# Narrow expert's tiles first in the experts' pool, and the first gate input split inside the GLU

## The chip, the cores and the metric

The kernel runs on one core of a Trainium2 chip. The metric is the device time of one execution in microseconds (us). The engines are TensorE (PE, with its weight loads PEld), VectorE (DVE), ScalarE (ACT), GpSimd (POOL) and SyncE (SP). Here SP and POOL start the DMA transfers, each in its own queue; the gathers by an index table are started by POOL.

## The reference

One layer of a decoder trunk, 2048 tokens of width 1024, float32:

```
h   = RMSNorm(x)
[u | q | k | v] = h @ W_in
yA  = S5 state-space model on u, GELU, then y * sigmoid(y @ w_glu + b_glu)
yB  = causal sliding-window attention (128) on q, k, v, 8 heads, sinks, relative bias
g   = sigmoid(h @ W_gate + b)
x  += (gA * (yA @ W_A) + gB * (yB @ W_B)) @ W_out
x  += HierMoE(RMSNorm(x))       32 experts of width 512, two per token
x  += (p @ W_ple) * sigmoid(RMSNorm(x) @ W_pg + b)
out = RMSNorm(x)
```

An attention step computes s = 0.125 * scores + bias, m = max(max(s), sink), exp(s - m) with its sum, and divides by the sum plus exp(sink - m).

## The kernel before

Every matrix product is made of three matmuls (lines 73 to 75): each float32 operand is split into a rounded high half (a cast on ACT) and a low half (a subtraction on DVE), and the products high x high, low x high and high x low are added up in PSUM. So every matrix that comes from memory costs a load, an ACT cast and a DVE subtraction before PE can use it.

The stages follow each other in program order, each overlapping the next at its edges: the u projection (to 122 us), q, k and v with pieces of the S5 model (to 343), the GLU (to 397), the gates' branch A (426 to 775), branch B (to 1048), the output projection (to 1257), the routing tables with the last pieces of the p projection (to 1300), the experts (1323 to 2084), and the last residual with its norm (to 2308).

- **Order.** A tile framework fixes each engine's instruction order when the program is built. Instructions of one engine, and the DMA starts of one queue, run in that order.
- **Memory.** Tiles live in pools; pools stack up from the left and from the right end of SBUF. A pool that is opened where another was closed takes its place, and a tile waits only for the work on those earlier tiles whose bytes it takes. Inside a pool the tiles lie in the order in which they are first asked for. The same tag with `bufs=n` rotates over n places.
- **u projection** (`u_mm`). Per block of 256 tokens, `scale` makes the row norms `rp` by a matmul (L459), copies them from PSUM to `rb` (ACT, L460, 8 of them), stores `rb`, and the eviction multiplies the block's products by `rb` into `ut` (DVE, L465). The q, k, v units are told to stay behind `self.scaled`, the last scaling instructions. The x halves for the next block are `xh` (ACT, L417) and `xl` (DVE, L418).
- **GLU and attention** (`phase_mix`). `weave` runs a generator of main steps and, after each, a fraction of steps of a second generator. The GLU has 16 steps (4 column blocks c, 4 output blocks m); its result goes into `ys` (L613), which is stored by 8 transfers after the last step (L619: one by SP, seven by POOL). The attention has 32 steps, 16 pairs of 128-token blocks and 2 key heads; 0.4 of a step runs per GLU step, 1.2 per step of branch A. In an attention step DVE takes the max of the scores (L820), ACT the exponentials with their sums (L829), DVE the reciprocal (L831), and POOL multiplies (L832). m, es and dn are tiles of 4 numbers per partition with two places each.
- **Gates, branch A** (`gates(c2, 0, 1)`). 32 steps: 2 halves of the columns, 8 token blocks e, 2 column groups. A step takes 48 matmuls `gz` (h times the gate weights gA) and 24 matmuls `gb` (y times bA), then tanh into `th` (ACT), the product into `mo` (DVE), and a store. For the first block both `gz` products come ahead of the `gb` products. The h halves come from `load_halves` (two loads, two casts, two subtractions per block; tiles `gh0000`, `gh0001` for the first block, whose raw loads go into a raw pool apart), the y halves `gy` from the stored `ys`. The first block's halves are asked for after the GLU's pools are closed. The gates' pools pB and pBh are opened on the left side where the GLU's lay; pB's first tiles, `bgate` among them, lie on `ys`.
- **Experts** (`moe`). 16 pairs of a wide expert (more than 128 token rows) and a narrow one. `moe_in` gathers the rows of one expert from memory into `xg` (L1356, tile names `xgs...`), PE transposes them (L1366, `txs`), ACT and DVE split them into `xw` (wide) or xh and xl (narrow). The gather's row numbers come from `row_index` (L1344 to L1348). After the first fetch all engines branch on a count (`overflow`, L1550). The experts' pool pM begins at byte 149,344 of a partition, worked out from the tile sizes; its tiles lie in the order of first use: `xw` (14,336 bytes), `xg` (2 of 4,096), then the rest. The three `po` tiles of the p projection before it, which are stored by `pp_d<-po` (L1070), were at 162,656 to 174,944.
- **Tail.** The pool of the last stage begins at the same byte 149,344; its first tile is `gtail` (8,192 bytes).

Of the kernel before, what the change touches and what calls it, by code (L numbers as in the profile page):

```python
# [11 lines left out]
F32 = mybir.dt.float32  # L12
F32R = mybir.dt.float32r
# [15 lines left out]
RM = 224  # L29
# [19 lines left out]
class Kern:  # L49
# [10 lines left out]
    @staticmethod  # L60
    def weave(main, fill, rate):

        due = 0.0
        for _ in main:
            due += rate
            while due >= 1.0:
                due -= 1.0
                if next(fill, "end") == "end":
                    due = -1e9
# [278 lines left out]
    def phase_mix(self):  # L348
        with ExitStack() as cA:
            att = self.attention(cA)  # L350
            with ExitStack() as c2:
                self.weave(self.glu(c2), att, 0.4)
            self.hlB = self.weight_pools()
            with ExitStack() as c2:
                self.weave(self.gates(c2, 0, 1), att, 1.2)
            for _ in att:
                pass
        with ExitStack() as c2:
            for _ in self.gates(c2, 1, 2):
                pass  # L360
# [75 lines left out]
    def u_mm(self, e, hk, ss, p1, p2, ps, wu, ut):  # L436
# [16 lines left out]
        def scale():  # L453
# [6 lines left out]
            self.scaled = dv.ins, nc.scalar.copy(rb, rp).ins  # L460
# [125 lines left out]
    def glu(self, ctx):  # L586
# [12 lines left out]
        for c in range(4):  # L599
# [7 lines left out]
            for m in range(4):  # L607
                z = ps.tile([128, 512], F32, tag="z", name=f"z{c}{m}")
                for k in range(4):
# [5 lines left out]
                                       in1=yk[:, m].rearrange("p (i n) -> p i n", i=4), op0=ALU.add, op1=ALU.mult)  # L615
                yield
# [101 lines left out]
    def attention(self, ctx):  # L718
# [80 lines left out]
        for e in range(8):  # L799
            (kh, kl), qs, vs, kn = nxt  # L800
            for w in range(2):
# [4 lines left out]
                for kv in range(2):  # L806
# [12 lines left out]
                    m = p.tile([128, 4], F32, tag="m", name=f"m{e}{w}{kv}")  # L819
# [4 lines left out]
                    es = p.tile([128, 4], F32, tag="es", name=f"es{e}{w}{kv}")  # L824
                    V.tensor_tensor(out=es, in0=sk, in1=m, op=ALU.add)
                    A.activation(es, es, AF.Exp)
                    dn = p.tile([128, 4], F32, tag="dn", name=f"dn{e}{w}{kv}")
# [15 lines left out]
    def gates(self, ctx, br, nb):  # L843
# [3 lines left out]
        hl = self.hlB  # L847
# [5 lines left out]
        ph = self.pool(ctx, "pBh", 1, side=side)  # L853
        ps = self.pool(ctx, "psB", nb, space=PSUM, side=side)
        bg = p.tile([128, 16], F32, name="bgate", bufs=1)
        nc.sync.dma_start(bg, I["b_gate"])
# [11 lines left out]
        if br == 0:  # L868

            pad = ph.tile([128, 4, 256], F32R, tag="hh", name="hpad", bufs=3)  # L870
            nc.gpsimd.memset(pad[0:1, 0, 0:1].bitcast(F32), 0.0)
        ahead = None if br else halves(0, 0, 0)
        wt = self.wB if br else weights(0)
        for h in range(2):
            for e in range(8):
# [3 lines left out]
                yh, yl = self.load_half(p if br else ph, ysrc, "y", f"gy{br}{h}{e}", nb, 2 if br else 0)  # L879
# [613 lines left out]
    def moe(self):  # L1493
        nc = self.nc
        self.yb_d = self.scratch("yb_d", [2 * T + 1, 1024])
        order = []
# [279 lines left out]
```

## Time and profile before

| | us |
|---|---|
| median of 3 runs | 2310.47 |
| lowest, highest | 2309.33, 2317.18 |
| the profiled execution | 2310.56 |
| its span | 2308.8 |
| PE busy in it | 2215.5 |
| DVE busy | 1659.7 |
| ACT busy | 1209.8 |
| POOL busy | 364.7 |
| mean granted clock of PE | 0.981 |

The span is the time from the first to the last recorded instruction; the execution's own time is 1.8 us longer. "Granted clock" is the share of TensorE's full speed that it was given. Idle time of an engine is put down to its releaser, the work whose end let it go on.

### The profile page before, as it was taken

To read this page: it belongs to the slowest core of one execution; us is meant where nothing else is said; L and a number is where in the kernel's file an instruction comes from. 1 tells how busy PE (TensorE), PEld (TensorE's weight loads), DVE (VectorE), ACT (ScalarE), POOL (GpSimd) and SP (SyncE) were. 2 spreads that over 40 slices of the span, in tenths; PEclk is the share of its full clock that TensorE was granted. 3 is DMA by queue.
4 is the path that set the end of the run, shared out by engine and by line. 5 is a ranking of instruction groups with operands and counts; after the bars stand their busy time and mean duration, and the time that the engine had idled before them with its cause. 6 is when DMAs were issued, how large, how long until landed. Compare 5 with 4: busy or idle time off the path is not lost. (4 is left out here: it accounts for less than half of the span.)

```text
span 2308.8 us, 38073 instructions
## 1 busy us (share of the span) xinstructions
PE 2215.5 (96%) x14524; PEld 1997.4 (87%) x14524; DVE 1659.7 (72%) x2915; ACT 1209.8 (52%) x2019; POOL 364.7 (16%) x282
## 2 busy tenths in 40 slices
PE   8889999899999999999999599999999999999997
PEld 8789997799999999998887488888898888887875
DVE  7878647888886434435666577787778888887997
ACT  6433335576665323322223466666667767764443
POOL 0043201221210000000001111122122211210212
PEclk9899999899999999999999799999999999999998
DMA  8485453644436456545553688889888998886562
GB/s 308 135 279 180 152 155 107 232 142 143 138 115 210 152 165 199 195 132 173 169 158 124 242 300 294 295 315 340 326 308 323 342 332 312 329 323 233 199 211 92
DMA packets 135321, 512.51 MB, mean 222 GB/s; under 512 B 16416, under 2 KB 34768, under 8 KB 107744
## 3 DMA queue, kind: packets, MB, share of 16 engines
q1 hardware_dynamic: 112544, 429.56, 54.6%
q0 software_dynamic: 22448, 80.23, 9.2%
q8 instruction: 115, 1.88, 0.3%
q14 instruction: 70, 0.57, 0.1%
q10 hardware_dynamic: 144, 0.26, 0.0%
HBM read 405.51 MB, written 101.20 MB: 219 GB/s over the span
## 5 line engine op out<-in xcount | busy, mean ns | idle before, releaser
L1481 DVE TENSOR_TENSOR e_l<-e_r,e_h 128x2048 fp32r<-128x2048 f32 x192 | 438.1, 2289 | 142.7 <-ACT e_h L1480 139.6
L1480 ACT CAST e_h<-e_r 128x2048 fp32r<-128x2048 f32 x192 | 366.5, 1910 | 140.5 <-PE ws L1405 39.9
L1405 PE MATMUL ws<-xw,e_h 128*128 128x320 f32 (+2 forms) x1024 | 290.5, 359 | 3.6 <-PEq L1550 3.6
L1406 PE MATMUL ws<-xw,e_l 128*128 128x160 f32 (+2 forms) x1024 | 251.8, 248 | 0.0
L1405 PEld LDWEIGHTS ws<-xw,e_h 128*128 128x128 f32 x1024 | 192.2, 189 | 7.6 <-issue 3.9
L1406 PEld LDWEIGHTS ws<-xw,e_l 128*128 128x128 f32 x1024 | 195.9, 192 | 0.0
L1356 POOL DMA_INDIRECT xgs<-h_d,rt x48 | 78.6, 1638 | 420.6 <-PE txs L1366 385.1
L1456 POOL DMA_INDIRECT yb_d<-yos,rt x48 | 79.9, 1664 | 214.3 <-DVE yos L1452 135.2
L832 POOL TENSOR_TENSOR s<-s,dn 128x1024 f32<-128x1024 f32 (+1 forms) x32 | 64.4, 2013 | 276.0 <-DVE dn L831 149.5
L75 PE MATMUL pz<-pg_h,pl 128*128 128x512 f32 (+1 forms) x264 | 103.1, 391 | 3.0 <-DVE pl L1611 3.0
L73 PE MATMUL gus<-e_h,xhs 128*128 128x512 f32 x256 | 102.9, 402 | 0.0
L75 PE MATMUL gus<-e_h,xls 128*128 128x512 f32 x256 | 102.7, 401 | 0.0
L73 PE MATMUL pz<-pg_h,ph 128*128 128x512 f32 (+1 forms) x264 | 101.6, 385 | 1.0 <-ACT ph L1610 1.0
L74 PE MATMUL gus<-e_l,xhs 128*128 128x512 f32 x256 | 101.6, 397 | 0.0
L74 PE MATMUL pz<-pg_l,ph 128*128 128x512 f32 (+1 forms) x264 | 101.3, 384 | 0.0
L73 PE MATMUL u<-xh,u_h 128*128 128x256 f32 x256 | 72.8, 291 | 18.5 <-DVE ut L465 9.8
L829 ACT ACTIVATE s<-s,m 128x256 f32<-128x256 f32 (+1 forms) x128 | 62.7, 492 | 36.5 <-DVE m L823 34.4
L74 PE MATMUL u<-xl,u_h 128*128 128x256 f32 x256 | 73.6, 291 | 0.0
L75 PE MATMUL u<-xh,u_l 128*128 128x256 f32 x256 | 72.8, 287 | 0.0
L1366 PE MATMUL txs<-ident,xgs 128*128 128x128 f32 (+3 forms) x384 | 48.8, 264 | 23.4 <-DMA xgs<-h_d,rt 22.8
L916 ACT ACTIVATE gt<-gz,bgate 128x256 f32<-128x256 f32 x128 | 53.4, 469 | 29.5 <-PE gz L75 26.2
L1366 PEld LDWEIGHTS txs<-ident,xgs 128*128 128x128 f32 (+3 forms) x384 | 40.8, 143 | 31.0 <-issue 27.3
(1489 smaller groups left out, 7366.5 us busy)
## 6 DMA issues: line engine op xcount, KB each, us to landing
e_r<-in_We SPq DMA_DIRECT2D x192, 1024.0 KB, 5.8
m_d<-mo SPq DMA_DIRECT2D x64, 256.0 KB, 3.7
yg<-yb_d SPq DMA_DIRECT2D x15, 1024.0 KB, 7.3
xt<-in_xT SPq DMA_DIRECT2D x16, 512.0 KB, 8.5
sq<-in_x SPq DMA_DIRECT2D x16, 512.0 KB, 5.4
m<-m_d SPq DMA_DIRECT2D x16, 512.0 KB, 5.0
xr<-in_x SPq DMA_DIRECT2D x16, 512.0 KB, 4.4
x_d<-xr POOLq DMA_DIRECT2D x16, 512.0 KB, 3.1
```

What stands on the lines that cost most here:

```text
L73: mm(out, ah, bh, start=start, stop=False)
L74: mm(out, ah, bl, start=False, stop=False)
L75: return mm(out, al, bh, start=False, stop=stop)
L829: A.activation(s[:, i], s[:, i], AF.Exp, bias=m[:, i:i + 1], accum_out=dn[:, i:i + 1])
L832: nc.gpsimd.tensor_tensor(out=s, in0=s, in1=dn.unsqueeze(2).to_broadcast([128, 4, n]), op=ALU.mult)
L1356: nc.gpsimd.indirect_dma_start(out=xg[0:rows], out_offset=None, in_=self.h2_d[:], in_offset=bass.IndirectOffsetOnAxis(ap=idx[0:rows], axis=0))
L1366: nc.tensor.transpose(tp[:, k], xg[0:rows, kk * 128:kk * 128 + 128], self.ident[0:rows, 0:rows])
L1405: mm(acc[b].rearrange("p (a n) -> p a n", a=2), wh[:, c:c + 128], xk, start=s, stop=False)
L1406: mm(acc[b][:, 0:n], wl[:, c:c + 128], xk[:, 0], start=False, stop=e)
L1456: nc.gpsimd.indirect_dma_start(out=self.yb_d[:], out_offset=bass.IndirectOffsetOnAxis(ap=d[0:rows], axis=0), in_=yo[0:rows], in_offset=None)
L1480: nc.scalar.copy(hi, raw)
L1481: nc.vector.tensor_tensor(out=lo, in0=raw, in1=hi, op=ALU.subtract)
```

## The change

Five edits:

1. In `u_mm.scale` the copy of `rp` to `rb` moves from ACT to DVE.
2. `weave` takes a set of steps: the attention now gets 0.5 step after each of the first 10 GLU steps and none in the last six (5 steps instead of 6 in all), and 1.2 steps after each step of branch A from the third on.
3. At GLU step 11, (c, m) = (2, 2), a pool `pAh` for h halves is opened on the right side, beside the attention's pool, and the first block's loads, casts and subtractions are issued there. Branch A uses that pool for all its h halves. The y halves move into pB, whose first tiles are now bgate, th, mo, half and a pad of 2,016 bytes, so that these lie on `ys` and the y halves begin where `ys` ends. The tile `hpad` and its memset are gone.
4. m, es and dn of an attention step become three parts of one tile `med` with one place (`bufs=1`).
5. `moe` asks first for the narrow expert's tiles (xh, xl, act, ah, al, aw: 29,696 bytes), so that `xw` and `xg` lie that much further on. Worked out from the sizes, they are then at 179,040 to 201,568, where the tables of the routing were.

```diff
--- before.py
+++ after.py
@@ -58,10 +58,12 @@
         return ctx.enter_context(self.tc.tile_pool(**kw))
 
     @staticmethod
-    def weave(main, fill, rate):
+    def weave(main, fill, rate, steps=range(1 << 20)):
 
         due = 0.0
-        for _ in main:
+        for n, _ in enumerate(main):
+            if n not in steps:
+                continue
             due += rate
             while due >= 1.0:
                 due -= 1.0
@@ -348,11 +350,13 @@
     def phase_mix(self):
         with ExitStack() as cA:
             att = self.attention(cA)
+            cB = ExitStack()
             with ExitStack() as c2:
-                self.weave(self.glu(c2), att, 0.4)
+                self.weave(self.glu(c2, cB), att, 0.5, range(10))
             self.hlB = self.weight_pools()
             with ExitStack() as c2:
-                self.weave(self.gates(c2, 0, 1), att, 1.2)
+                self.weave(self.gates(c2, 0, 1), att, 1.2, range(2, 32))
+            cB.close()
             for _ in att:
                 pass
         with ExitStack() as c2:
@@ -457,7 +461,7 @@
                 dg = p1.tile([128, 128], F32, tag="dg", name=f"dg{e}{a}", bufs=2)
                 dv = V.tensor_scalar(out=dg, in0=self.ident, scalar1=rs[:, a:a + 1], scalar2=None, op0=ALU.mult)
                 nc.tensor.matmul(rp[:, a * 128:a * 128 + 128], self.ones, dg, start=True, stop=True)
-            self.scaled = dv.ins, nc.scalar.copy(rb, rp).ins
+            self.scaled = dv.ins, V.tensor_copy(rb, rp).ins
             nc.sync.dma_start(self.rb_d[e], rb)
 
         def evict(mp):
@@ -583,7 +587,7 @@
         yield
 
 
-    def glu(self, ctx):
+    def glu(self, ctx, cB):
         tc, nc, I = self.tc, self.nc, self.I
         V, A = nc.vector, nc.scalar
 
@@ -613,6 +617,10 @@
                 V.scalar_tensor_tensor(out=ys[:, m, :, c * 4:c * 4 + 4].rearrange("p n i -> p i n"),
                                        in0=z.rearrange("p (i n) -> p i n", i=4), scalar=1.0,
                                        in1=yk[:, m].rearrange("p (i n) -> p i n", i=4), op0=ALU.add, op1=ALU.mult)
+                if (c, m) == (2, 2):
+
+                    self.phA = self.pool(cB, "pAh", 1, side="right")
+                    self.ahA = self.load_halves(self.phA, self.hT[0], "h", "gh000", raws=0)
                 yield
         for e in range(8):
             q = nc.gpsimd if e else nc.sync
@@ -816,15 +824,14 @@
                     s = p.tile([128, 4, 256], F32, tag="s", name=f"s{e}{w}{kv}")[:, :, 0:n]
                     V.scalar_tensor_tensor(out=s, in0=sc[:, :, 0:n], scalar=0.125,
                                            in1=bias[:, kv * 4:kv * 4 + 4, 256 - n:256], op0=ALU.mult, op1=ALU.add)
-                    m = p.tile([128, 4], F32, tag="m", name=f"m{e}{w}{kv}")
+                    med = p.tile([128, 3, 4], F32, tag="m", name=f"m{e}{w}{kv}", bufs=1)
+                    m, es, dn = (med[:, q] for q in range(3))
                     V.tensor_reduce(out=m, in_=s, axis=AX, op=ALU.max)
                     sk = sink[:, kv * 4:kv * 4 + 4]
                     V.tensor_tensor(out=m, in0=m, in1=sk, op=ALU.max)
                     V.tensor_scalar(out=m, in0=m, scalar1=-1.0, scalar2=None, op0=ALU.mult)
-                    es = p.tile([128, 4], F32, tag="es", name=f"es{e}{w}{kv}")
                     V.tensor_tensor(out=es, in0=sk, in1=m, op=ALU.add)
                     A.activation(es, es, AF.Exp)
-                    dn = p.tile([128, 4], F32, tag="dn", name=f"dn{e}{w}{kv}")
                     for i in range(4):
                         A.activation(s[:, i], s[:, i], AF.Exp, bias=m[:, i:i + 1], accum_out=dn[:, i:i + 1])
                     V.tensor_tensor(out=dn, in0=dn, in1=es, op=ALU.add)
@@ -850,9 +857,14 @@
             self.m_d = self.scratches("m_d", 8, [128, 8, 256])
         side = "right" if br else "left"
         p = self.pool(ctx, "pB", 1, side=side)
-        ph = self.pool(ctx, "pBh", 1, side=side)
+        ph = self.pool(ctx, "pBh", 1, side=side) if br else self.phA
         ps = self.pool(ctx, "psB", nb, space=PSUM, side=side)
         bg = p.tile([128, 16], F32, name="bgate", bufs=1)
+        if br == 0:
+
+            for t, b in (("th", 1), ("mo", 2), ("half", 2)):
+                p.tile([128, 2 if b == 1 or t == "mo" else 4, 256], F32, tag=t, name=f"{t}at", bufs=b)
+            p.tile([128, 504], F32, tag="pad", name="pad", bufs=1)
         nc.sync.dma_start(bg, I["b_gate"])
         V.tensor_scalar(out=bg, in0=bg, scalar1=0.5, scalar2=None, op0=ALU.mult)
         dst = self.m_d if br else self.m1_d
@@ -865,18 +877,14 @@
         def halves(h, e, raws=2):
             return self.load_halves(ph, self.hT[e], "h", f"gh{br}{h}{e}", raws=raws, rp=p)
 
-        if br == 0:
-
-            pad = ph.tile([128, 4, 256], F32R, tag="hh", name="hpad", bufs=3)
-            nc.gpsimd.memset(pad[0:1, 0, 0:1].bitcast(F32), 0.0)
-        ahead = None if br else halves(0, 0, 0)
+        ahead = None if br else self.ahA
         wt = self.wB if br else weights(0)
         for h in range(2):
             for e in range(8):
                 hk = ahead or halves(h, e)
                 ahead = None
                 ysrc = self.ya_d[e] if br else self.ys_d[e]
-                yh, yl = self.load_half(p if br else ph, ysrc, "y", f"gy{br}{h}{e}", nb, 2 if br else 0)
+                yh, yl = self.load_half(p, ysrc, "y", f"gy{br}{h}{e}", nb, 2 if br else 0)
                 hs = slice(4 * h, 4 * h + 4)
                 if br:
                     m1 = p.tile([128, 4, 256], F32, tag="m1", name=f"m1{h}{e}")
@@ -1493,6 +1501,14 @@
     def moe(self):
         nc = self.nc
         self.yb_d = self.scratch("yb_d", [2 * T + 1, 1024])
+
+        p = self.mp
+        for q in "hl":
+            p.tile([128, 8, 128], F32R, tag=f"x{q}", name=f"x{q}at", bufs=1)
+        p.tile([128, 512], F32, tag="act", name="aat", bufs=3)
+        for q in "hl":
+            p.tile([128, 4, 128], F32R, tag=f"a{q}", name=f"a{q}at", bufs=2)
+        p.tile([128, 4, 2 * RM], F32R, tag="aw", name="awat", bufs=1)
         order = []
         for i in range(16):
             order += [(i, [i, 32 + i]), (31 - i, [31 - i])]
```

## Rows read from the trace of the kernel before

**Rows 1.** Engine table of the page: busy us, share of the span, instructions.

```profile
PE 2215.5 (96%) x14524; PEld 1997.4 (87%) x14524; DVE 1659.7 (72%) x2915; ACT 1209.8 (52%) x2019; POOL 364.7 (16%) x282
```

**Rows 2.** Windows: us; busy us of PE, PEld, DVE, ACT, POOL; granted clock; DMA share; GB/s.

```profile
400.00:425.00 25.00, 13.37 (x49) 10.85 (x50) 22.48 (x35) 18.51 (x39) 9.06 (x10) 0.54 0.77 267
...
450.00:475.00 25.00, 25.00 (x208) 24.59 (x207) 21.08 (x33) 16.67 (x38) 5.31 (x3) 1.00 0.31 96
...
1300.00:1325.00 25.00, 5.87 (x24) 4.94 (x25) 2.50 (x4) 4.40 (x6) 3.83 (x4) 0.50 0.69 252
```

**Rows 3.** Timeline at the MoE's start: start us, us, engine, line, operation [idle before <-releaser].

```profile
1292.78 0.19 DVE L1347 TENSOR_SCALAR rt<-rt 128x48 int32<-128x48 int32 x1
...
1292.88 6.69 DVE L1481 TENSOR_TENSOR e_l<-e_r,e_h 128x2048 fp32r<-128x2048 f32 x3
...
1305.32 1.02 POOL L1356 DMA_INDIRECT xgs<-h_d,rt  x1 [22.32 <-DMA pp_d<-po]
...
1314.82 1.94 PE L1366 MATMUL txs<-ident,xgs 128*128 128x128 f32 x8 [22.78 <-DMA xgs<-h_d,rt]
...
1322.71 0.71 PE L1405 MATMUL ws<-xw,e_h 128*128 128x448 f32 x1 [3.64 <-PEq L1550]
```

**Rows 4.** Windows of 5 us before the MoE.

```profile
1295.00:1300.00 5.00, 0.00 (x0) 0.00 (x0) 4.57 (x3) 2.83 (x5) 0.00 (x0) 0.64 0.00 2
...
1305.00:1310.00 5.00, 0.00 (x0) 0.00 (x0) 0.00 (x0) 0.00 (x0) 1.96 (x2) 0.50 0.98 411
```

**Rows 5.** All instructions of the tile xgs, MoE: ns min/median/max, first and last start.

```profile
L1356 POOL DMA_INDIRECT xgs<-h_d,rt x48: 917/1638/2499, 1305.3 to 2011.0; - x48
...
DMA to landing us min/median/max: 4.2/7.2/11.5
```

**Rows 6.** Timeline from the GLU to the gates.

```profile
397.31 0.39 PE L75 MATMUL z<-yh,glu_l 128*128 128x512 f32 x1
...
406.71 2.34 DVE L90 TENSOR_TENSOR gA_l<-gA_r,gA_h 128x1024 fp32r<-128x1024 f32 x2
...
422.91 1.05 ACT L632 CAST gh0000h<-gh0000r 128x1024 fp32r<-128x1024 f32 x1
...
424.43 0.33 SPq L856 DMA_DIRECT2D bgate<-in_b_gate  x1
...
426.27 0.40 PE L73 MATMUL gz<-gh0000h,gA_h 128*128 128x256 f32 x2
...
441.40 0.36 PE L73 MATMUL gz<-gh0010h,gA_h 128*128 128x256 f32 x1
```

**Rows 7.** Windows of 395 to 430 us, their sum.

```profile
sum 35.00, PE 21.17 PEld 17.51 DVE 30.01 ACT 24.74 POOL 12.96; mean PE 3.02 PEld 2.50 DVE 4.29 ACT 3.53 POOL 1.85
```

**Rows 8.** Timeline at 60 to 70 us, and all of the tile rb.

```profile
63.92 1.22 DVE L418 TENSOR_TENSOR xl<-xt,xh 128x1024 fp32r<-128x1024 f32 x1
...
68.60 0.55 PE L73 MATMUL u<-xh,u_h 128*128 128x256 f32 x1 [9.77 <-DVE ut L465]
...
L460 ACT COPY rb<-rp x8: 353/372/373, 30.3 to 117.5; 128x256 f32<-128x256 f32 x8
```

**Rows 9.** All L820 of the attention, and the timeline of one step.

```profile
L820 DVE TENSOR_REDUCE m<-s x32: 648/1209/1224, 373.0 to 696.5; 128x4 f32<-128x1024 f32 x30, 128x4 f32<-128x512 f32 x2
...
413.57 1.21 DVE L820 TENSOR_REDUCE m<-s 128x4 f32<-128x1024 f32 x1
...
426.01 3.90 POOL L832 TENSOR_TENSOR s<-s,dn 128x1024 f32<-128x1024 f32 x1 [1.42 <-DVE dn L831]
```

**Rows 10.** Timeline of PE at the attention's end and at branch A's end.

```profile
717.47 0.47 PE L755 MATMUL pv<-ph,vs 128*128 128x512 f32 x1 [0.70 <-DVE ya L758]
...
763.78 0.28 PE L73 MATMUL gb<-gy017h,bA_h 128*128 128x256 f32 x1
```

**Rows 11.** Timeline of SP and DVE at the MoE's tail.

```profile
2094.37 0.36 SPq L1660 DMA_DIRECT2D gtail<-in_g_tail  x1
...
2109.41 0.75 DVE L1636 SCALAR_TENSOR_TENSOR pth<-pz,prs0y,gtail 128x512 f32<-128x512 f32 x1 [2.45 <-PE pz L75]
```

## Prediction

> **What bounds the kernel now.** I read the engine table first: PE is busy for nearly the whole span [rows 1], so an edit pays only where PE stands still or runs at a low granted clock. The windows of 25 us say where that is. Of the three rows shown, the middle one is what almost every window between 450 and 2075 us looks like: PE busy throughout. The other two are the holes next to which the diff works: 400 to 425 (13.37 us busy at 0.54 of the clock) and 1300 to 1325 (5.87 us busy at 0.50) [rows 2]. A third, smaller hole is at 60 to 70 us. Then, per hole, the waits and the timeline: which instruction PE stood before, and what that instruction's releaser was itself waiting for. The diff adds no matmul, so inside the full windows it can cost only by making PE wait.
>
> **The MoE's start (part: pool order).** PE's longest wait before the experts is 22.78 us for `xgs`, the first gathered tokens. The timeline gives the chain: the gather's row numbers are ready on DVE at 1292.97 (L1347: 1292.78 + 0.19), but POOL issues the gather at 1305.32, after 22.32 us idle, released by a store `pp_d<-po`; first transpose 1314.82; first expert matmul 1322.71 [rows 3]. The store matters only because `xg` lies on `po`'s bytes: pM starts at 149,344 (worked out from the tile sizes), `xw` takes 14,336 bytes, so the two `xg` tiles are at 163,680 to 171,872, inside the three `po` tiles at 162,656 to 174,944. With 29,696 bytes of narrow-expert tiles placed first, `xw` and `xg` move to 179,040 to 201,568, over routing tables whose last reader is the row-number arithmetic itself. What then lies over `po` is first written for the narrow expert, a full wide expert later: that stall is covered.
>
> New chain: gather at about 1293.1. Landing: before it took 9.5 us to the first transpose (1305.32 to 1314.82 [rows 3]), with the DMA engines 0.98 busy in 1305 to 1310; in 1295 to 1300 they are idle (0.00) [rows 4]. Over the 48 gathers the landing is 4.2 us at least, 7.2 in the middle [rows 5]. I take 5.5 us, between the least and the middle, because the engines are free from 1295 on: transposes at 1298.6. From first transpose to first expert matmul it was 7.89 us (1314.82 to 1322.71), which includes the branch on the overflow count that all engines take; kept, the experts start at 1306.5 instead of 1322.7: **16 us**. Ends: a landing of 9.5 us gives 12, one of 4.2 gives 17.5. Behind it PE is fed: three of the first expert's four weight units are split before 1299.6 (three subtractions, 6.69 us from 1292.88 [rows 3]).
>
> A point against it: POOL would now issue while DVE does those subtractions; before, DVE was idle. The 48 issues take 917 ns at least, 1638 in the middle, 2499 at most [rows 5], so two of them cost at most 3 us more than two like the 1.02 us one at 1305.32; inside the bounds above. The Trainium skill bears on this ("SBUF — State Buffer", sections "SBUF: two separate sides" and "Who interferes with whom"): GpSimd and VectorE share a port pair as a lock, and a DMA from the GpSimd queue can starve because its descriptors can't be written, though the page leaves two-input operations like this subtraction out of that and calls the reason inferred. What the lock would cost here, if it held all the same, stands with the rivals.
>
> **From the GLU to the gates (parts: early h halves, `pAh`, pB's places, weave).** The last GLU matmul is at 397.31, the first gate matmul at 426.27 [rows 6]. Over 395 to 430 PE is busy for 21.17 of 35 us [rows 7], mostly at half clock. The gates' first input is late because its casts come only after the GLU's pools close and `ys` is stored: ACT casts `gh0000h` at 422.91 and PE starts 3.4 us later [rows 6]. The change issues those two loads, casts and subtractions at GLU step 11 into places that are free by then (the q, k, v pool and the bias tables, both done with). They cost ACT 2 x 1.05 us and DVE about as much, moved from the stalled stretch into the GLU's end. PE's gate matmuls then wait for the gate weights alone, whose last two low halves end on DVE at 409.05 (406.71 + 2.34 [rows 6]).
>
> What can run early: a step's gate product is 48 matmuls of 128x256. A full window has 208 matmuls in 25 us [rows 2], 0.12 us each, so a step's product is 5.8 us and both steps on the first input 11.5. The branch product needs `gy`, hence all of `ys` stored and read back. The second input is not early either: its raw tiles in pB lie on `ys`, whose stores have landed by 424.43, when `bgate`, the first tile there, is loaded [rows 6]. So 11.5 us of gate work moves into a gap with 13.8 us idle, and the second input's product, at 441.40 before, can come at 428 to 430. I take **12 us**: the 11.5, and a little because PE is busier and its clock comes up earlier. Low end 4: the gate products go in at half clock and push the attention's own matmuls back, so that about a third is left; high end 16, the 13.8 idle and two of clock.
>
> **The u projection (part: `rb` on DVE).** PE stands 9.77 us before 68.60 until DVE has evicted `ut`, which needs `rb` from a busy ACT [rows 8]. The copies (8 x 0.37 us) leave ACT and DVE gets 3.0 us. DVE is full there too, and PE's next unit also needs `xl` (63.92 + 1.22, then a second of 1.21): with `rb` and four `ut` (0.7 + 2.1 us) put ahead of it, `xl` ends near 68, next to no gain; with `ut` and `xl` ahead of other S5 work up to 4.5. The whole wait, 9.8, is the bound. I take **2 us**, nearer to no gain, as DVE has no slack.
>
> **One tile for m, es, dn (`bufs=1`).** The next attention step's max (L820) must now wait for this step's multiply on POOL (L832). L820 starts 32 times between 373.0 and 696.5, a period of 323.5/31 = 10.4 us [rows 9]. From a step's L820 to the end of its L832 the timeline gives 6.3 to 16.3 us (the longest: 413.57 to 429.91 [rows 9]), about 11 in the middle; in 13 of 31 pairs the next L820 started before that end. So the period grows to perhaps 11 to 12 us. The waiting L820 sits in DVE's order, and behind it stand halves and evictions of the gates. The cover: attention's last matmuls are near 717, and branch A's gate products end at 763.78 [rows 10]; 27 steps from 430 may take 12.3 us each. I put **+1 us** for short stalls of PE, 0 to 5. One attention step fewer in the GLU moves about as much PE work as it removes: 0.
>
> **The tail.** `gtail` now lies on tiles of the last projection pass instead of `xw`, so its load (2094.37) comes some 3 us later, SP's loads behind it too; first use at 2109.41, after DVE had waited 2.45 us for PE [rows 11]: **+1**, 0 to 2.
>
> **Sum.** 2310.56 (the profiled run, within 0.1 us of the median 2310.47) - 16 - 12 - 2 + 1 + 1 = 2282.6, say 2283. All terms at their good ends: 2310.6 - 17.5 - 16 - 9.8 = 2267. All at their bad ends: 2310.6 - 12 - 4 + 5 + 2 = 2302.
>
> **Rivals.**
> 1. *The gates' start gains little.* DVE is busy for 30.01 of the 35 us around it [rows 7]; if DVE, not the input, sets when the stretch ends, the term is 4 and not 12: 2291. Against: the two subtractions moved away were part of just that DVE time.
> 2. *The gather waits for DVE.* Descriptors only at 1299.57, plus 5.5 and 7.9: experts at 1313.0, a term of 10: 2289. For: the longest issue, 2499 ns, is about as long as one such subtraction. Against: half of the issues took under 1.64 us.
> 3. *The gather is not freed.* Another reader under the new places, or the order of POOL's queue, holds it at 1305 as now: term 0, 2299.
> 4. *Slower: attention outlasts branch A.* Mechanism: the single m/es/dn tile. If a step's period is p, attention ends at 430 + 27p and branch B waits for it past 763. At 12.3 us it costs nothing; each further us costs 27. It eats the 28 us gained at 13.4, and at 14 the time is about 2328. For: 11 us of chain in the middle leaves little room. Against: the long chains are long because other work lay between, with no wait on them; the short ones take 6.3.
>
> **Chances.** 0.55 for the sum as worked out (its own range 2274 to 2291), 0.17 for rival 1, 0.08 for rival 2, 0.07 for rival 3, 0.13 for rival 4, of which half ends above 2317. A measurement here tells 0.3% (7 us) from nothing, so faster means below 2303.5. Slower 0.07 (half of rival 4), within 0.3% 0.07 (part of rivals 3 and 4), faster 0.86. The range 2268 to 2303 leaves out some 0.13 above and 0.05 below.
>
> **What would show it.** Right: the gather issued at about 1293 with no wait for `pp_d`; expert matmuls from 1306; `gz` matmuls between 400 and 420 and PE busier there; the wait before `u` shorter. Wrong: POOL still released by `pp_d`; PE waiting on `gh001` or `gy000` until 440; waits on `pt` or `ya` between 700 and 780; windows in branch A with less than 24 us of PE in 25.

## The result, and the profile after

Median of four runs 2275.91 us (2272.36 to 2278.26) against 2311.09 (2309.33 to 2317.18) for the kernel before: ratio 0.9842, 95% interval 0.982 to 0.9864. The profiled execution has a span of 2274.3 us against 2308.8. The forecast was 2283 in 2268 to 2303: right in direction and size. But its term for the MoE's start was 4 us too large, 11 us came from a place that the sum did not have, and two of its terms came out together and not each by itself.

Where the 34.5 us of span went, by the first or last instruction of a tile in both traces (minus is earlier; the last column is the difference to the line above):

| mark | before | after | shift | gained here |
|---|---|---|---|---|
| first GLU matmul `z` | 343.6 | 341.5 | -2.1 | -2.1 |
| last gate product of branch B (`mo<-gt,gb`, on DVE) | 1047.7 | 1034.1 | -13.6 | -11.5 |
| first expert matmul `ws` | 1322.7 | 1297.2 | -25.5 | -11.9 |
| last `ys<-ahs` of the experts | 2083.1 | 2046.8 | -36.3 | -10.8 |
| end | 2308.8 | 2274.3 | -34.5 | +1.8 |

The engine table of the page after, and its windows (length, then busy us with instruction count for PE, PEld, DVE, ACT and POOL, granted clock, DMA share, GB/s). The first and third are the holes of [rows 2]:

```profile
PE 2202.4 (97%) x14524; PEld 1994.3 (88%) x14524; DVE 1651.0 (73%) x2923; ACT 1208.2 (53%) x2011; POOL 364.3 (16%) x281
```

```profile
400.00:425.00 25.00, 21.25 (x155) 19.27 (x154) 19.55 (x31) 14.93 (x37) 7.47 (x7) 0.95 0.97 340
...
1275.00:1300.00 25.00, 9.70 (x65) 8.01 (x64) 11.79 (x14) 14.48 (x16) 5.93 (x4) 0.66 0.82 304
1300.00:1325.00 25.00, 25.00 (x156) 23.32 (x156) 19.91 (x25) 19.17 (x28) 1.85 (x2) 1.00 0.83 297
```

The hole at 400 is nearly filled: 21.25 busy instead of 13.37, at a granted clock of 0.95 instead of 0.54. The one at the MoE's start lies a window earlier and is shallower.

Timeline of the changed kernel at the MoE's start (start, us, engine, line, operation, tiles; idle before it and its releaser), to be read against [rows 3]:

```profile
1279.58 0.19 DVE L1355 TENSOR_SCALAR rt<-rt 128x48 int32<-128x48 int32 x1
1279.68 6.69 DVE L1489 TENSOR_TENSOR e_l<-e_r,e_h 128x2048 fp32r<-128x2048 f32 x3
1280.61 2.24 POOL L1364 DMA_INDIRECT xgs<-h_d,rt  x1 [10.83 <-issue]
...
1283.15 1.83 POOL L1364 DMA_INDIRECT xgs<-h_d,rt  x1 [0.30 <-issue]
...
1286.35 1.94 PE L1374 MATMUL txs<-ident,xgs 128*128 128x128 f32 x8 [7.51 <-DMA xgs<-h_d,rt]
1287.42 5.55 SPq L1479 DMA_DIRECT2D e_r<-in_We  x4
...
1290.57 1.20 DVE L1376 TENSOR_TENSOR xw<-txs,xw 128x384 fp32r<-128x384 f32 x2 [0.94 <-ACT xw L1375]
...
1297.24 0.71 PE L1413 MATMUL ws<-xw,e_h 128*128 128x448 f32 x1 [6.58 <-PEq L1566]
```

The gather no longer waits for `pp_d`: it is issued 0.84 us after the row numbers (1279.58 + 0.19 to 1280.61), before 12.35. The first transpose comes 5.74 us later, before 9.50. But from there to the first expert matmul it is 10.89 us instead of 7.89, and PE's wait names its own queue at L1566, the overflow branch.

Timeline of the changed kernel from the GLU's step 11 to the gates, against [rows 6]; then from its list of the tile `gz` the second input (count, shortest, median and longest ns, first and last start):

```profile
378.84 1.04 ACT L640 CAST gh0000h<-gh0000r 128x1024 fp32r<-128x1024 f32 x1
...
398.24 0.38 PE L75 MATMUL gz<-gh0000h,gA_h 128*128 128x256 f32 x1 [3.59 <-DVE ys L617]
...
424.05 1.05 ACT L640 CAST gh0010h<-gh0010r 128x1024 fp32r<-128x1024 f32 x1
```

```profile
L75 PE MATMUL gz<-gh0010h,gA_h x16: 278/279/387, 425.1 to 444.2; 128*128 128x256 f32 x16
```

The first input is cast inside the GLU, and the first gate matmul starts at 398.24 instead of 426.27, after 3.59 us of waiting for the GLU's last result in `ys`; the second input's first product comes at 425.1, before 441.40. The window of [rows 7], after:

```profile
sum 35.00, PE 27.23 PEld 25.04 DVE 29.10 ACT 22.58 POOL 10.02; mean PE 27.23 PEld 25.04 DVE 29.10 ACT 22.58 POOL 10.02
```

PE has 6 us more work in the 35, DVE almost the same. Timeline of the changed kernel before the block of u of [rows 8], whose wait was 9.77 us:

```profile
59.74 0.36 PE L75 MATMUL u<-xh,u_h 128*128 128x256 f32 x1 [1.33 <-DVE ut L469]
```

The attention's maxima of the changed kernel, against [rows 9], and DVE's wait for POOL in 400 to 720 us (total, times, longest):

```profile
L829 DVE TENSOR_REDUCE m<-s x32: 680/1220/1223, 369.7 to 717.8; 128x4 f32<-128x1024 f32 x30, 128x4 f32<-128x512 f32 x2
```

```profile
DVE m L829 <- POOL s L839: 13.9, 12, 2.1
```

The single `m` tile does make DVE wait, 12 times. The period grows from 10.4 to 11.2 us (348.1/31), but in the run with two places below it is 11.1 too, so that growth is not the single place's. From the third step on the attention's maxima come 6 to 21 us later than before; the gate products come 28 us earlier at the first token block, 16 to 23 at the next ones and 13.5 at the last, and branch A as a whole ends 13.5 us earlier.

### The profile page after: what moved, and what is told of

Its sections match the earlier page's. It is cut to its first block, busy times and chain, and to the rows that moved or that the text cites. A ratio compares the mean times of both kernels' runs of the same rounds, so it can differ in the third digit from the quotient of the medians.

```text
span 2274.3 us, 38003 instructions
## 1 busy us (share of the span) xinstructions
PE 2202.4 (97%) x14524; PEld 1994.3 (88%) x14524; DVE 1651.0 (73%) x2923; ACT 1208.2 (53%) x2011; POOL 364.3 (16%) x281
## 3 DMA queue, kind: packets, MB, share of 16 engines
q8 instruction: 115, 1.88, 0.3%
## 5 line engine op out<-in xcount | busy, mean ns | idle before, releaser
L1364 POOL DMA_INDIRECT xgs<-h_d,rt x48 | 87.0, 1812 | 392.6 <-PE txs L1374 366.1
L839 POOL TENSOR_TENSOR s<-s,m 128x1024 f32<-128x1024 f32 (+1 forms) x32 | 59.7, 1865 | 313.9 <-DVE m L838 248.1
L1671 POOL TENSOR_TENSOR pth<-pth,gtail 128x1024 f32<-128x1024 f32 x15 | 36.4, 2425 | 176.4 <-ACT pth L1670 151.6
L77 PEld LDWEIGHTS pz<-pg_h,pl 128*128 128x128 f32 x264 | 49.9, 189 | 15.5 <-DVE pl L1627 6.5
```

Source lines behind the costliest of these rows:

```text
L77: return mm(out, al, bh, start=False, stop=stop)
L839: nc.gpsimd.tensor_tensor(out=s, in0=s, in1=dn.unsqueeze(2).to_broadcast([128, 4, n]), op=ALU.mult)
L1364: nc.gpsimd.indirect_dma_start(out=xg[0:rows], out_offset=None, in_=self.h2_d[:], in_offset=bass.IndirectOffsetOnAxis(ap=idx[0:rows], axis=0))
```

## The experiments

All ratios are against the kernel before on the same chip.

**Each group of edits alone.** *Pool order alone* (before, plus the lines in `moe`):

```diff
 def moe(self):
+    p = self.mp
+    ...            # xh, xl, act, ah, al, aw asked for first, as in the change
```

> The kernel before with the new pool order alone. Comparing the two traces, three things seem to come from it: the experts start 12 us earlier (the gather no longer waits for the store), the expert stage itself is 11 us shorter (the narrow expert's matmuls start 227 ns apart and not 234), the tail is 2 us longer. Theory: all three are the pool order's, so 2310.5 - 12 - 11 + 2 = 2289.5, and the interval of the narrow matmuls is 227 ns. Rival: the shorter expert stage comes from the other parts; then only the start and the tail move, 2300, and the interval stays at 234.

Measured: 2289.57 us (2287.49 to 2293.53), ratio 0.9904 (0.9883 to 0.9925). The start of the experts gains 12.5 us, and the expert stage itself, in which the prediction expected no change, 10 us more. The tail does not lose the 2 us that this run's theory gave to the pool order.

*The eviction of `rb` alone:*

```diff
-            self.scaled = dv.ins, nc.scalar.copy(rb, rp).ins
+            self.scaled = dv.ins, V.tensor_copy(rb, rp).ins
```

> The kernel before with the rb copy on DVE alone. The change's trace is 5 us ahead at the end of the u projection and 2 to 3 us ahead when the GLU begins. Theory: those 2 to 3 us are this part's and stay to the end: 2308. Rivals: they are lost again at the GLU's end, where DVE and not PE sets the time (2310.5); or all 5 stay when the later stages are as before (2305.5).

Measured: 2307.32 us (ten runs, 2302.32 to 2311.36), ratio 0.9976 (0.9964 to 0.9989). The trace is 4.2 us ahead at the GLU's first matmul, 4.7 at the experts' end, and loses 2.3 after that.

*The GLU and gates part alone* (the change without the pool order and with `rb` back on ACT):

```diff
-            self.scaled = dv.ins, V.tensor_copy(rb, rp).ins
+            self.scaled = dv.ins, nc.scalar.copy(rb, rp).ins
 def moe(self):
-    p = self.mp
-    ...
```

> The kernel before with the early first h halves, the weave's new steps, the single m/es/dn tile and pB's new places; rb on ACT and the experts' pool as before. In the change's trace the stretch from the GLU's end to branch B gains 10.5 us. Theory: these parts give it on their own: 2300. Rival: part of it came because DVE was ahead from the u projection on; then 2304 or more. If all three edits add up, e1, e2 and e3 together give the 35 us of the change.

Measured: 2299.03 us (2296.68 to 2303.48), ratio 0.9945 (0.9923 to 0.9967): 0.5 us ahead at the GLU's first matmul, 11.9 at branch B's end. The product of the three ratios is 0.9826, the change's 0.9842: within their intervals the three groups add up, and no large term is left that only their company makes. Inside the GLU and gates part it is otherwise, as the runs with one tile for m, es, dn show.

**Why the experts themselves became faster.** A matmul with a stationary tile of 128x128 from the narrow expert's tiles took 397 ns before and 389 after, and the starts, in an unbroken run of them, are 234 and 227 ns apart, both at a granted clock of 1.00. The pool order moved those tiles from bytes 178,112 to 194,496 of each partition down to 149,344 to 171,872 (worked out from the tile sizes). The wide expert's `aw`, the stationary tile of its own `ys` matmuls, went from 202,688 to 209,856 down to 171,872 to 179,040, and its matmuls became faster in the same way. Two kernels bring one pair to the other side.

*xh, xl up again, the others low* (in the change):

```diff
-    for q in "hl":
-        p.tile([128, 8, 128], F32R, tag=f"x{q}", name=f"x{q}at", bufs=1)
+    p.tile([128, 1024], F32, tag="yo", name="yoat")
+    p.tile([128, 4, 2 * RM], F32R, tag="aw", name="awat", bufs=1)
     ...            # act, ah, al
-    p.tile([128, 4, 2 * RM], F32R, tag="aw", name="awat", bufs=1)
+    p.tile([128, 8, 2, RM], F32R, tag="xw", name="xwat", bufs=1)
+    p.tile([128, 1024], F32, tag="xg", name="xgat")
```

> The changed kernel with another order of the experts' pool: xw and xg at the same bytes as in the change (179,040 to 201,568, so the gather is as free), but the narrow expert's xh and xl behind them (201,664 to 209,856) and ah, al at 170,848 to 179,040. Theory, place: the narrow expert's matmuls are quicker where their xh and xl lie low; then gus goes back from 227 to 234 ns (768 x 7 ns = 5 us), ys is unsure (0 to 5 us), the experts' start as in the change, the tail 2 us better: 2279 to 2284. Rival, gather: the intervals shortened because the gather and what follows it come earlier, or because of where xw and xg lie; then 227 stays and the time is 2274 to 2276.

*xh, xl low, the others where they were* (in the kernel before):

```diff
 def moe(self):
+    for q in "hl":
+        p.tile([128, 8, 128], F32R, tag=f"x{q}", name=f"x{q}at", bufs=1)
```

> The kernel before with xh and xl alone at the start of the experts' pool; ah and al stay at 186,304 to 194,496 and aw at 202,688, xg comes to 171,872 to 180,064, still touching the last of the three po tiles. Theory, place: gus falls to 227 ns and ys stays at 234: the expert stage is 5 us shorter, the tail 2 us longer, and the start moves only as far as that po tile is stored earlier: 2298 to 2308. Rival, gather: both stay at 234 as long as the gather is held; if it is freed, both fall to 227.

Measured: 2282.71 us, ratio 0.9871 (0.9853 to 0.9889), and 2301.13, ratio 0.9955 (0.9942 to 0.9968). The rows of three matmul groups (the narrow expert's `gus` and `ys`, and the wide expert's `ys`) of before, of the change, of the first and of the second experiment (count, shortest/median/longest ns):

```profile
L73 PE MATMUL gus<-e_h,xhs x256: 391/397/505, 1346.6 to 2065.8; 128*128 128x512 f32 x128
L73 PE MATMUL ys<-e_h,aws x160: 391/398/400, 1358.6 to 2073.2; 128*128 128x512 f32 x128, 128*96 128x512 f32 x32
...
L73 PE MATMUL ys<-e_h,ahs x128: 392/398/496, 1391.1 to 2083.1; 128*128 128x512 f32 x128
```

```profile
L75 PE MATMUL gus<-e_h,xhs x256: 389/389/501, 1320.4 to 2029.8; 128*128 128x512 f32 x128
L75 PE MATMUL ys<-e_h,aws x160: 387/389/397, 1332.1 to 2037.1; 128*128 128x512 f32 x128, 128*96 128x512 f32 x32
...
L75 PE MATMUL ys<-e_h,ahs x128: 389/389/499, 1364.5 to 2046.8; 128*128 128x512 f32 x128
```

```profile
L75 PE MATMUL gus<-e_h,xhs x256: 392/397/505, 1321.7 to 2036.2; 128*128 128x512 f32 x128
L75 PE MATMUL ys<-e_h,aws x160: 387/389/398, 1333.7 to 2043.5; 128*128 128x512 f32 x128, 128*96 128x512 f32 x32
...
L75 PE MATMUL ys<-e_h,ahs x128: 389/389/499, 1366.1 to 2053.3; 128*128 128x512 f32 x128
```

```profile
L73 PE MATMUL gus<-e_h,xhs x256: 389/389/501, 1340.5 to 2054.8; 128*128 128x512 f32 x128
L73 PE MATMUL ys<-e_h,aws x160: 391/397/400, 1352.2 to 2062.3; 128*128 128x512 f32 x128, 128*96 128x512 f32 x32
...
L73 PE MATMUL ys<-e_h,ahs x128: 392/398/496, 1384.7 to 2072.2; 128*128 128x512 f32 x128
```

Each group follows the place of its own stationary tile: `xh`, `xl` are low in the second and fourth, `ah`, `al` and `aw` in the second and third. With `xh`, `xl` back up the expert stage is 6.3 us longer than in the change; with only these low it is 5.3 shorter than before. That agrees with 768 `gus` matmuls of 7 ns (5.4 us). The narrow `ys` (384 matmuls, 2.7 us) and the wide `ys` at the full width (448, 3.1 us) bring the sum to 11.2, beside 10.8 in the table above. Over all runs each pair that ended at 180,064 or below was fast; pairs at 178,112 to 186,304, at 186,304 to 194,496 and at 201,664 to 209,856 were slow. Why is open; no run moved the expert weights, the other operand, so whether the byte itself counts or its place against theirs is not separated.

**The one tile for m, es, dn.** *Two places in the change; in the kernel before, the single tile alone; and the change with one place but the attention's pool 64 bytes longer, as two places make it, up to the rounding:*

```diff
-    med = p.tile([128, 3, 4], F32, tag="m", name=..., bufs=1)
+    med = p.tile([128, 3, 4], F32, tag="m", name=..., bufs=2)   # two places; pad 504 -> 488
```

```diff
-    m = p.tile([128, 4], F32, tag="m", name=...)
+    med = p.tile([128, 3, 4], F32, tag="m", name=..., bufs=1)   # alone, in the kernel before
+    m, es, dn = (med[:, q] for q in range(3))
```

```diff
+    p.tile([128, 16], F32, name="gap", bufs=1)                  # 64 bytes; pad 504 -> 488
```

> The changed kernel with two places for the tile of m, es and dn (and 64 bytes less of the pad, so that it fits). In the change's trace attention's matmuls come 8 to 15 us later than before during branch A while the gates' come 20 us earlier. Theory: PE is busy throughout branch A, so the single place costs nothing but order: 2275 to 2277. Rival: the wait of L820's successor for POOL stalls DVE and through it PE; then two places give 3 us or more: 2273 or less.

> The kernel before with m, es and dn in one tile with one place, and nothing else. Two places in the changed kernel cost 8 to 10 us. Theory 1: one place gives an order that is better by itself, so the kernel before gains 5 to 10 us too: 2301 to 2306. Theory 2: two places hurt only together with the early gate input, whose matmuls then compete with attention's; alone one place does nothing: 2309 to 2312. My forecast's own term for it was a loss of 0 to 5 us: 2311 to 2316.

> The changed kernel, m/es/dn with one place as in the change, but with everything else that the run with two places changed: 64 unused bytes in the attention's pool, so that pAh lies 64 bytes lower, the pad 64 bytes shorter, and the y halves begin on ys's last 64 bytes. It tells which of the two cost the 8 us. Theory 1, the bytes: the first y half now waits for all of ys's stores, and that was the loss: 2283 to 2286. Theory 2, the places: two places let attention's steps run closer together against the gates, and that was the loss: 2275 to 2277 here.

Measured: two places 2284.34 us, ratio 0.9872 (0.9848 to 0.9896), 8 slower than the change; the single tile alone 2319.21 (eight runs), ratio 1.0039 (1.0027 to 1.005), 8 slower than before; the 64 bytes 2277.84, ratio 0.9849 (0.983 to 0.9867), as the change. The first two lie outside everything that was expected of them; the third speaks for the places. Windows of the three in that order:

```profile
400.00:425.00 25.00, 17.82 (x127) 16.02 (x127) 19.44 (x33) 14.92 (x43) 8.54 (x7) 0.91 0.82 296
...
500.00:525.00 25.00, 22.70 (x189) 22.28 (x188) 21.47 (x30) 17.98 (x39) 5.68 (x3) 1.00 0.49 156
```

```profile
400.00:425.00 25.00, 10.22 (x42) 7.92 (x43) 18.82 (x29) 15.87 (x33) 8.98 (x9) 0.69 0.69 246
425.00:450.00 25.00, 22.41 (x148) 20.72 (x148) 15.48 (x23) 12.67 (x31) 3.88 (x3) 0.77 0.64 211
```

```profile
400.00:425.00 25.00, 21.31 (x148) 19.80 (x148) 18.57 (x31) 13.70 (x34) 6.07 (x6) 0.86 0.91 323
```

Much of the loss sits in the same stretch each time: PE is busy for 17.82 us with two places beside 21.25 in the change, and for 10.22 with the single tile alone beside 13.37 before [rows 2]. It is not all there: with two places PE stands 2.3 us more in 500 to 525, and with the single tile alone 425 to 450 still has a granted clock of 0.77, before 0.98. So one place costs 8 us without the early halves and brings 8 with them, and it is not the bytes. The two comparisons are not quite the same edit: the run of the single tile alone also makes one tile out of three, and one tile with two places in the kernel before was not run. What of its 8 us is the place and what the merging is open.

How much the early halves bring by themselves can be read from the last gate product of branch B, here with `rb` alone and with two places in the change:

```profile
L918 DVE SCALAR_TENSOR_TENSOR mo<-gt,gb x64: 666/680/690, 438.8 to 1043.9; 128x512 f32<-128x512 f32 x64
```

```profile
L926 DVE SCALAR_TENSOR_TENSOR mo<-gt,gb x64: 668/680/690, 430.8 to 1041.9; 128x512 f32<-128x512 f32 x64
```

Both have `rb` on DVE; only the second has the early halves (with the weave's new steps), and it is 2.0 us ahead. The change, with one place, is at 1034.1. The timed runs agree: the ratio of two places, 0.9872, is 0.9992 of the product of pool order and `rb` alone (0.9904 x 0.9976), about 2 us, although their intervals allow some 8 us to either side.

PE's waits of the single tile alone in 397 to 450 us show who comes late there:

```profile
PE sc L814 <- DVE s L817: 7.2, 2, 3.9
PE vt L784 <- DVE ya L758: 5.0, 1, 5.0
```

Before, the same two waits were 1.8 and 3.0 us. PE waits for DVE's attention work, in an order fixed at build time. What that order does when a tile has one place or two is not settled further.

**The weave.** The change with the old shares:

```diff
-                self.weave(self.glu(c2, cB), att, 0.5, range(10))
+                self.weave(self.glu(c2, cB), att, 0.4)
...
-                self.weave(self.gates(c2, 0, 1), att, 1.2, range(2, 32))
+                self.weave(self.gates(c2, 0, 1), att, 1.2)
```

> The changed kernel with the weave's old rates (0.4 per GLU step over all 16, 1.2 from branch A's first step on). Theory: attention steps in the GLU's last six steps and in branch A's first two take DVE and ACT time from the first gate input and from the y halves, so 2 to 6 us are lost: 2278 to 2282. Rival: the early halves alone make the gain and the weave is worth nothing: 2275 to 2277.

Measured: 2275.05 us (2272.56 to 2278.25), ratio 0.9829 (0.9805 to 0.9852): the same as the change, as this run's rival had it. Nothing of the 2 to 6 us of its theory shows; the prediction had put the weave at 0.

**The three us lost at the MoE's start.** PE's own branch instruction (ns, start) in before, the change, the pool order alone and the GLU part alone, each with the window of its duration:

```profile
L1550 PEldq COMPARE_BRANCH  x1: 3786/3786/3786, 1318.8 to 1318.8; - x1
...
1318.80:1322.59 3.79, 0.27 (x2) 0.00 (x0) 1.12 (x2) 0.53 (x2) 0.94 (x1) 0.50 0.41 106
```

```profile
L1566 PEldq COMPARE_BRANCH  x1: 6786/6786/6786, 1290.3 to 1290.3; - x1
...
1290.30:1297.09 6.79, 0.36 (x3) 0.07 (x1) 1.11 (x2) 0.72 (x2) 0.94 (x1) 0.50 1.01 379
```

```profile
L1558 PEldq COMPARE_BRANCH  x1: 6526/6526/6526, 1303.5 to 1303.5; - x1
...
1303.50:1310.03 6.53, 0.14 (x1) 0.00 (x0) 0.99 (x2) 0.48 (x1) 0.94 (x1) 0.50 0.99 379
```

```profile
L1558 PEldq COMPARE_BRANCH  x1: 3806/3806/3806, 1305.6 to 1305.6; - x1
...
1305.60:1309.41 3.81, 0.26 (x2) 0.00 (x0) 1.12 (x2) 0.52 (x2) 0.94 (x1) 0.50 0.41 110
```

The branch takes 3.8 us where the DMA engines are 0.41 busy and 6.5 to 6.8 where they are full (last column but one). In each stretch one packet of the page's instruction queue q8 moves (115 packets, 1.88 MB: 16 KB each). Before, the expert weights (`e_r`, issued from 1302.00) had landed before the branch; now their loads, issued from 1287.42 on, run beside it. The reading is that PE's code comes through the same engines; that is argued from durations and packets, not isolated.

Two kernels put the branch ahead of the first transposes, so that its time passes while the gather lands; the second also orders the weight casts of the first two experts behind those of `xw`:

```diff
+    got = [self.moe_gather(...) for s, w in ...]     # the first two gathers
     ...                                              # the overflow branch
-    cur = v, fetch(order[0][1])                      # was ahead of the branch
+    cur = v, fetch(s0, got)
```

```diff
+    with self.tc.issue_after(first[0]), self.tc.issue_after(first[1]):
+        wt = ahead + [self.moe_split(*w) for w in raws]
```

> The changed kernel with the branch on the overflow count moved between the first gathers and their transposes (its own gather, never run here, takes xw's place for its rows). In the change's trace PE's branch takes 6.8 us, against 3.8 before, because it runs after the transposes while the weight loads fill the DMA engines; the experts then wait for it 5.4 us after xw is ready. Theory: the branch now runs while the gather is in flight, and the experts start when xw is ready: 5 us off, 2271. Rival: the gather or the transposes wait for the branch instead: 2274 to 2277.

> The kernel with the branch moved between the first gathers and their transposes, now with the casts and subtractions of the next weight units ordered behind those of xw on ACT and DVE. With the branch moved alone, ACT stood 10.5 us for a weight load that its order put ahead of xw's cast, and the experts started 10 us later. Theory: that order was the loss, and with it mended the experts start when xw is ready, 5 us before the change: 2271. Rival: the transposes still wait for something behind the branch; 2276 or more.

Measured: 2285.09 us, ratio 0.9871 (0.9849 to 0.9894), and 2278.5, ratio 0.9867 (0.985 to 0.9883): nothing gained, the first one loses more than either expectation allowed, and the second is its rival's case. In both PE's branch falls out of the path, and something else fills the time. Timeline of ACT in the first, then of PE in the second:

```profile
1293.16 1.28 ACT L1498 ACT_TABLE_LOAD   x1 [10.54 <-DMA e_r<-in_We]
...
1298.73 1.06 ACT L1385 CAST xw<-txs 128x512 fp32r<-128x512 f32 x2
```

```profile
1284.41 1.94 PE L1384 MATMUL txs<-ident,xgs 128*128 128x128 f32 x8 [7.84 <-DVEq L1585]
...
1296.17 1.08 PE L1384 MATMUL txs<-ident,xgs 128*128 128x128 f32 x4 [6.40 <-DMA xgs<-h_d,rt]
1296.91 0.72 PE L1424 MATMUL ws<-xw,e_h 128*128 128x448 f32 x1
```

In the first the order puts a weight cast ahead of the `xw` casts, and ACT stands 10.54 us for that weight's load. In the second `xw` is ready near 1291, but the narrow expert's transposes stand ahead of the first expert matmul on PE and wait 6.40 us for their gather: 1296.91, within 0.4 us of the change.

**The tail.** The change with `aw` and a 1,024-byte pad ahead of the narrow tiles, so that `gtail` lies on tiles that end sooner:

```diff
+    p.tile([128, 4, 2 * RM], F32R, tag="aw", name="awat", bufs=1)
+    p.tile([128, 256], F32, tag="pad", name="padat", bufs=1)
     ...            # xh, xl, act, ah, al
```

> The changed kernel with aw (7,168 bytes) and a pad of 1,024 first in the experts' pool, then xh, xl, act, ah, al as in the change; the tail's gtail then lies on aw, whose last reader is done some 20 us before. Theory: gtail's load no longer waits for the projection's tiles, and the 2 us that the tail lost come back: 2274; gus, ys stay at 227 ns, since ah and al end at 180,064. Rival: the tail's loss has another cause (2276), or ah and al are already too high at 171,872 to 180,064: ys at 230 to 234 ns, 2278 to 2280.

Measured: 2275.06 us (2273.59 to 2276.63), ratio 0.9842 (0.9825 to 0.9858). `gtail` is issued 1.8 us sooner (2058.6 instead of 2060.4) and nothing follows from it. From the last `ys<-ahs` to the first `pth` it is 26.3 us in the kernel before and with the pool order alone, 27.7 in the change, 28.6 with `rb` alone, 28.2 here. So the tail's loss does not come from the pool order. It goes with the first edit: 26.1 to 26.4 us in all five kernels with `rb` on ACT, 27.3 to 28.6 in all nine with it on DVE. DVE then stands a second time for `yg`, which is read back from memory: 0.67 us in the change, 1.32 with `rb` alone, not at all before. Why copies that are done by 118 us [rows 8] act there is open.

No version beats the change: the one without the weave and the one with `aw` first equal it.

## Why the prediction was right, point by point

1. *The MoE's start, -16.* From the row numbers to the first expert matmul 12.3 us were gained: 11.5 at the issue, 3.8 at the landing, and 3.0 given back. The landing of 5.5 was right (5.74), with the DMA engines 0.39 busy in 1280 to 1287 and not 0.98 as before. The step that failed is "kept" for the 7.89 us from transpose to expert matmul: the branch in it is no constant, it took 6.8 us instead of 3.8 at its earlier time, when the weight loads ran beside it; that these loads are the reason is argued above and not isolated. The sum would have been -13, near the bad end of that term. That the branch sat in the 7.89 was seen; what it would meet at the new time was not asked.
2. *The GLU to the gates, -12.* With the +1 of point 4 it is -11, measured -11.5 by the table above and -11.4 (11.9 less 0.5) in the experiment with this part alone. The sum of the two came out, and that is luck, for the split is wrong: without the single place the early halves bring 2 us by the trace, less than the 4 of rival 1, and the rest comes only with the single place. The second input came sooner than forecast, at 425.1 and not 428, though branch A then kept 13.5 of the 16 to 23 us by which its gate products led. The first gate product also did not wait for the gate weights alone, but for the GLU's last result in `ys`.
3. *The u projection, -2.* -2.1 at the first GLU matmul in the change, -4.2 in the experiment with `rb` alone. One trace does not resolve that; over all of them the mark lies at 343.1 to 346.6 in the five kernels with `rb` on ACT and at 338.9 to 341.5 in the nine with it on DVE, 3.7 us between the medians. By the ten timed runs with `rb` alone the edit is worth 2.5 to 8.3 us (0.11 to 0.36% of 2311), so 2 was small. The wait shrank from 9.77 to 1.33 us. At the last `u` matmul 5.0 us were left of that (116.44 instead of 121.42), after later waits of 1.1 to 1.9 us for `xl` and `ut`, and more was lost in q, k and v.
4. *One tile for m, es, dn, +1.* The waits came as described (12, at most 2.1 us each), but the period of 11.2 is not theirs, as it is 11.1 with two places. The trace of before has 15 pairs in which the next max starts before the multiply ends, not 13. As a price the term was wrong: +8 alone, with the merging of three tiles in it, and -8 beside the early halves. "A cost per step, hidden by slack at the end" was the wrong form; the runs show PE standing or slower mostly between 400 and 450 us, and why the place changes that is open.
5. *The tail, +1.* Measured +1.8, by luck: the reason given, `gtail`'s later load, is refuted, and the loss goes with the first edit.
6. *Not foreseen:* the expert stage, -10.8, from where the stationary tiles of the narrow and of the wide experts lie.

So 4 us too much for the start, set against 11 us that were not in the sum, leave the 7 by which the time came out lower.

The rivals: the gates' start gained in full in the change (1), but not without the single place. The gather did not wait for DVE (2): it was issued at 1280.61 under subtractions that ran from 1279.68 to 1286.37. The Trainium skill ("SBUF — State Buffer", sections "SBUF: two separate sides" and "Who interferes with whom") excepts a two-input `tensor_tensor` from the VectorE operations that stall a DMA started by GpSimd, though with both inputs in SBUF it contends with GpSimd's reads. The trace agrees with the exception: both gathers were issued before the subtractions ended. They took 2.24 and 1.83 us where the first took 1.02 in [rows 3] with DVE idle, the part of this rival that did come. The gather was freed (3). The attention fell behind but did not outlast branch A (4).

## What to carry to other kernels

A stall that is taken away moves what follows it beside other traffic: ask of each constant in the chain behind it, a branch above all, what it will run beside at the new time. The order in which a pool's tiles are asked for decides both which earlier work a first load waits for and where matmul operands lie, and both showed in this profile. Under an order that is built ahead, a resource such as a tile's second place had no price of its own here; it has to be measured in the company in which it will run. And a total that comes out says little about its terms: two edits in one stretch need a run with each of them left out.

## What the runs showed of the hardware that was not expected

- The interval between 128x512 matmuls was 227 or 234 ns with the place of the stationary tile in SBUF, at a granted clock of 1.00 in both. The wide expert's stationary `aw` showed the same step. Its transposed inputs `xw`, the moving operand of `ws`, showed none: starts were 213, 201 and 184 ns apart in the median at 448, 384 and 320 columns, with `xw` at 149,344 and at 179,040 alike.
- PE's compare-and-branch took 3.5 to 3.8 us in the three kernels in which the DMA engines were at most 0.41 busy, and 6.1 to 7.0 in the seven in which they were at least 0.94 busy. In the two kernels with the branch moved it took 0.37 us. In two more (the old weave, the single tile alone) it took 0.37 us as well, and PE still stood 5.5 and 3.4 us behind it, at a DMA share of 1.00 and 0.39; so the instruction's own duration is not the whole of it.
- The first two indirect gathers from POOL's queue took 2.2 and 1.8 us in nine kernels in which DVE was subtracting beside them, and 1.0 and 0.9 in four in which it was idle. In the kernel with only `xh`, `xl` low the first took 1.02 us although a subtraction ran, the second 1.80; so a running subtraction does not always slow them.
